# A two-layer hybrid trunk on one core: the first layer's shift and scale computed in two halves, with norm, transposes and weights placed between them

## The chip, the cores and the metric

The kernel runs on one core of a Trainium2 chip. The time is the device time of one execution in microseconds (us); the median of several executions is compared. Engine names are those of the profile: PE is TensorE's products, PEld its weight loads, DVE is VectorE, ACT is ScalarE, POOL is GpSimd, SP is the engine that issues the DMAs (SPq in the timeline, since issuing is work of its queue).

## The reference, cut to what matters

Two layers run one after the other over 1152 tokens (128 context tokens and 1024 latent tokens) of 1024 channels, in float32. At the head of each layer stands

```
m = silu(cvec) @ mod_w + mod_b          # 1024 -> 3 * 1024: shift, scale, gate
h = rmsnorm(x, norm_g) * (1 + scale) + shift
p = h @ w_in                            # one projection for all three branches
```

with one `cvec` for the context tokens and one for the latent tokens. The columns of `p` feed a windowed attention (A), a gated linear recurrence (B) and a differential attention (C), whose outputs are gated, projected, merged, projected again by `w_out` and added to `x` under `gate`. For this change only the first layer's way from `cvec` and `x` to the first columns of `p` matters.

## The kernel before, in words

**Tiling.** The 1152 tokens are nine tiles of 128 rows, handled in three chunks of three tiles. The 1024 channels are eight column blocks of 128 (`KT`, index k). `h` is kept transposed, as eight pairs `L.hh[k]`, `L.hl[k]`: each value split into a part rounded to the format of the fast products and the remainder, so that one exact product is three fast ones (`mm3`, L161 to L163 in the profile: high by high, high by low, low by high).

**Modulation of the first layer.** `mod_rows(D, b0, n)` computes n blocks of 128 columns of `m` on TensorE: four loads of 512 KB of `mod_w` (tile `modw`), eight products with 512 columns (L281; the trace shows two matmul instructions for each), one copy of the row to SBUF on ScalarE (`mrow`), four tiny transposes (L288), and two additions on VectorE into `D.modt`. It is a generator with a step per load. It is called for blocks 0 to 3 (shift, first half of the channels), 8 to 11 (scale, first half), 4 to 7 and 12 to 15 (second halves). Below, the first two calls are the first half of the modulation, the last two the second half. `mod_gs(D, k0, k1)` then makes the factor `norm_g * (1 + scale)` for column blocks k0 to k1.

**Norm.** `load_x(i)` loads one token tile (512 KB). `norm_x(c)` squares the three tiles of chunk c on ScalarE with row sums (L1142 in the profile), makes 1/sqrt by a dozen small VectorE operations (`rsqrt`, tile `rsq`), and scales the three tiles on VectorE.

**Into h.** `to_h(L, c, k, ...)` transposes column block k of the three tiles of chunk c on TensorE (three transposes, L332, into a PSUM buffer `ps_t`, of which there are three), applies factor and shift there (ScalarE, L337, or VectorE for k = 3 and 7), copies the rounded part out on ScalarE (tile `h`) and the remainder on VectorE.

**Projection weights.** `load_wu` loads three groups of 128 columns of `w_in` for all eight row blocks in nine DMAs (tile `wuraw`), and splits them into `uwh` (rounded copy, ScalarE) and `uwl` (remainder, by `split`'s last argument on VectorE or GpSimd) in three pieces. `tok_gemm(L, i, w)` then projects one token tile: for k = 0 to 7 one `mm3` into a PSUM buffer `ps_s`, of which there are four. `qkv_gemm` does so for three tiles and then copies queries, keys and values out.

**Order of the work.** The text of the kernel gives the instructions, a planner orders them. The context that the kernel is written in schedules all instructions at the end with a timeline of its own: an instruction written earlier has the higher priority (shifted where the code says `tc.high_priority`), and one that its inputs or buffers hold back can be passed by a later one. The result is a fixed order for each engine; at run time each engine takes its instructions in that order. All DMAs are issued from SP's queue. Large tiles share rings of buffers: ring S has 26 buffers, and `modw` (16 in all in this stretch), the nine tiles of `x` and the 16 tiles of `h` all come from it; ring W has 7 for the weights.

**The program's beginning, before.** The four calls of `mod_rows` stand one after the other; after the second one, tiles 0 to 2 of `x` are loaded and normalised and the first projection weights are loaded and split (`XPOS`, `WUK`). Then come both calls of `mod_gs`, the loads of tiles 3 to 8 with the rotation tables between them (`load_unit_consts`), `alloc_h`, and for each chunk its norm and eight calls of `to_h`. `unit_phase` follows with the first projection, `qkv_gemm` for unit 0.

Of the kernel before, what the change touches and what calls it, by code (L numbers as in the profile page):

```python
# [24 lines left out]
# priority offsets: attention of the units, branch products, modulation (beside the tail, w_out; its sums), recurrence  # L25
# [6 lines left out]
# chunks that branch products lag the merge; steps of the tail where they lag two  # L32
MLAG = 1
LAG2 = (7, 8)
# steps of the tail that carry a block of modulation, that carry a recurrence, that writes the states
# [3 lines left out]
# places in w_out that carry a block of modulation  # L39
MODW = ((0, 1), (0, 4), (0, 7), (1, 1), (1, 4), (1, 7), (2, 1), (2, 4))  # L40
# first layer: blocks of modulation after which the weights and the first tokens are loaded
WUK = 1
XPOS = 1
# rings of the rows of x in w_out, and in its last quarter
XT = 'EDT'
XT3 = 'ET'
# background products per group of query tiles: units of branch C, the first of them, branch A
# [3 lines left out]
# rings of shared buffers: how many of each  # L51
RINGS = {"S": 26, "P": 7, "T": 2, "Q": 2, "W": 7, "D": 3, "E": 2, "cx": 1, "tab": 1}

# columns of w_in
# [3 lines left out]
# rows of the per-layer table of short vectors  # L58
# [4 lines left out]
def hybrid_dit_kernel(ctx, tc, I, O):  # L63
# [5 lines left out]
    # buffers of each kind in PSUM  # L69
# [8 lines left out]
    def al(tag, name, *shape):  # L78
        """a buffer of one of the shared rings"""
        return big.tile([128] + list(shape), F32, tag=tag, name=name, bufs=RINGS[tag])  # L80
# [41 lines left out]
    def rsqrt(x, n, scale, eps=None):  # L122
        """1/sqrt(x*scale + eps) of a [128, n] AP, n <= 12"""
        o = tl("rsq", 4, 12, bufs=3)
        ms, y, h, t = (o[:, i, 0:n] for i in range(4))
        if eps is None:
            ts(V, ms, x, scale, ALU.mult, EPS, ALU.add)
        else:
            stt(ms, x, scale, eps, ALU.mult, ALU.add)
        ts(V, y.bitcast(I32), ms.bitcast(I32), 1, ALU.logical_shift_right)  # L130
        ts(V, y.bitcast(I32), y.bitcast(I32), -1.0, ALU.mult, float(0x5F3759DF), ALU.add)
        ts(V, h, ms, -0.5, ALU.mult)
        for _ in range(3):
            tt(V, t, y, y, ALU.mult)
            tt(V, t, t, h, ALU.mult)
            stt(y, t, 1.5, y, ALU.add, ALU.mult)
        return y

    def split(hi, lo, raw, eh="A", el="P"):
        """hi = raw rounded to fp32r, lo = raw - hi"""  # L140
        if eh == "A":
            acopy(r(hi), raw)
        else:
            V.tensor_copy(r(hi), raw)
        tt(Pq if el == "P" else V, r(lo), raw, hi, ALU.subtract)

    def ws_load(wcols, kt):
        """[kt*128, 128] weight columns -> hi, lo [128, kt, 128]"""
# [29 lines left out]
    def ws_gemm(L, wcols, consume):  # L178
        """[128 cols, tokens] = W^T h^T, per chunk of 384 tokens"""
# [5 lines left out]
    def layer_vectors(l):  # L185
        """generator: loads the rows, two per step, then turns them into columns"""
# [25 lines left out]
    def layer_scalars(D):  # L212
# [12 lines left out]
        # lamc[3] = -(e1 - e2 + lam_init)  # L225
# [11 lines left out]
        # 4*softplus(-lam) = 4*(max(-lam, 0) + log1p(exp(-|lam|)))  # L237
# [21 lines left out]
    def silu_c():  # L259
        """[128, k, s]: silu of the two conditions, latent and context, in columns"""  # L260
# [13 lines left out]
    def mod_rows(D, b0, n):  # L274
        """blocks b0 to b0 + n by TensorE: the conditions' rows, then turned into columns; a step per load"""
# [17 lines left out]
    def mod_chunk(D, b0, n, tag):  # L293
        """blocks b0 to b0 + n: products summed over row blocks by DVE, over partitions by a product with ones"""
# [22 lines left out]
    def mod_gs(D, k0, k1):  # L317
        # gs = norm_g * (1 + scale); s = 0 latent, 1 context
# [8 lines left out]
    def to_h(L, c, k, xn, tags):  # L327
        """column block k of the normalised tiles of chunk c -> h^T, hi and lo"""
# [23 lines left out]
    def load_wu(L, groups, early=False):  # L352
        """three groups of 128 columns -> (hi, lo) [128, 384] for each of the 8 row blocks"""
# [3 lines left out]
        def conv(raw):  # L357
            m = raw.shape[1]
            hi, lo = al("W", "uwh", m, 384), al("W", "uwl", m, 384)
            split(hi, lo, raw, "A", "P")  # L360
# [19 lines left out]
    def qk_rows(L, i0, pss, gains, dsts, eng=None):  # L380
        """normalise, scale and rotate pairs of heads of a few token tiles.
        gains: gain index per pair; dsts: where a pair goes, None: stays in the returned tile"""
# [41 lines left out]
    def put_k(d0, d1, p):  # L424
        """p: [head 0; head 1] -> key stacks [hi; lo] of head 0 and [lo; hi] of head 1"""
# [6 lines left out]
    def q_conv(src, nb):  # L432
        """src [128, nb, 64] -> hi and lo of the transposed blocks, each in both halves: [2, nb, 128]"""
# [11 lines left out]
    def gate_silu(L, c0, put):  # L445
        """2*silu of the gate columns from c0"""
# [19 lines left out]
    def qkv_gemm(L, u, w, gains, okey, oval, eng=None):  # L466
        """generator: emits one third of the work per step"""
# [16 lines left out]
    def k_conv(u, cache, kdst):  # L484
        """keys transposed and stacked; kdst: destinations of key blocks b0..b0+n (8: cached)"""
# [16 lines left out]
    def v_conv(u, cache, pair=False):  # L502
        """values split: hi and lo, or for a pair of heads [hi; lo] of each"""
# [19 lines left out]
    def c_probs(L, u, i, q, t):  # L523
        """unnormalised difference of the two softmaxes of q tile i -> [128, n] in a P buffer"""
# [27 lines left out]
        # softmax_0 - lam softmax_1 = (e_0 - lam l_0/l_1 e_1) / l_0; the norm after it takes 1/l_0 into its eps  # L552
# [46 lines left out]
    # key blocks (8 is the cached context) in the two key rows of a head pair, and  # L599
    # for each latent block: row, first key slot, count, first mask slot  # L600
# [40 lines left out]
    def a_probs(L, g, tiles, q):  # L641
        """softmaxes of heads 2g, 2g+1 for one or two q tiles"""
# [83 lines left out]
    def unit_phase(L):  # L726
        """the four heads of branch C, then branch A; projections run beside the attention before them"""
# [24 lines left out]
        def background():  # L752
            """projections and gates, in the order in which attention takes them"""
# [78 lines left out]
    def lru_x(L, ct):  # L832
        """input of the recurrence and its gate, to DRAM"""
# [17 lines left out]
    def lru(L, ct):  # L851
# [5 lines left out]
        # gate matrices, two 64-wide blocks on the diagonal  # L857
# [76 lines left out]
    def load_o(L, br):  # L934
        """gated branch output, hi and lo"""
# [44 lines left out]
    def tail_step(L, br, order, j, o, lag):  # L980
        """emits the products of step (br, j) one chunk at a time, branch products MLAG chunks behind the merge"""
# [22 lines left out]
    def tail_last(L, br, ohl):  # L1004
        """the last two steps of the last branch: their merge products first, so that h can go"""
# [15 lines left out]
    def gate_rows(D, q4, dst):  # L1021
        """dst [2, 256]: gate/2 in every partition, latent and context"""
# [124 lines left out]
    for n, b0 in enumerate((0, 8, 4, 12)):  # L1147
        g = mod_rows(L.D, b0, 4)
        for _ in range(3):
            drive(vec, g)  # L1150
        for _ in vec:
            pass
        drive(g)
        if n == XPOS:
            for i in range(3):
                load_x(i)
            norm_x(0)
        if n == WUK:
            L.wu = load_wu(L, c_groups(0), True)
    mod_gs(L.D, 0, 4)  # L1160
    mod_gs(L.D, 4, 8)
    for i in range(3, 9):
# [3 lines left out]
    alloc_h(L)  # L1166
    for c in range(3):
        if c:
            norm_x(c)
        for k in range(KT):  # L1170
            to_h(L, c, k, lambda t, kk, c=c: xs[3 * c + t][:, kk * 128:(kk + 1) * 128], "t")
# [49 lines left out]
def _consts():  # L1221
    """arrays that depend on shapes alone"""
# [35 lines left out]
```

## Time and profile before

| | us |
|---|---|
| median of 3 executions | 2898.65 |
| lowest, highest | 2894.25, 2900.79 |
| span of the profiled execution | 2896.5 |
| TensorE busy in it | 2741.7 (95%) |
| VectorE, ScalarE, GpSimd busy | 1753.5, 1272.5, 908.3 |

The page gives no time for the profiled execution other than its span, from the first instruction to the last; it lies 2.15 us below the median. In a timeline each row has the start, the time during which instructions of this group ran, engine, line, operation, output and inputs, shape and count; brackets hold the idle time of the engine just before and what ended it. A row of a table by windows has the busy time of each engine (with its number of instructions) in the stretch, the granted TensorE clock (1.00 is the upper of two levels, 2.4 GHz, 0.50 the lower, 1.2 GHz), the busy share of the DMA engines and the bytes they moved.

### The profile page before, as it was taken

What the parts mean: (1) busy time and instruction counts of PE and PEld (TensorE: products, weight loads), DVE (VectorE), ACT (ScalarE), POOL (GpSimd) and SP (SyncE); (2) the same over time, 40 slices, a digit from 0 to 9 for tenths busy, and PEclk for the clock granted to TensorE, in tenths of its full rate; (3) what the DMA queues carried; (4) which work ended last, traced back from release to release, by engine and by line L of the source; (5) the groups of instructions that cost most, each with busy time, mean ns of one, the idle gap of its engine ahead of it and who ended that gap; (6) DMA issues with size and microseconds to landing.
All of it is one profiled execution on the core that took longest, in us unless ns stands there. A gap on an engine that the chain in (4) does not pass through costs nothing.

```text
span 2896.5 us, 44162 instructions
## 1 busy us (share of the span) xinstructions
PE 2741.7 (95%) x16745; PEld 2651.9 (92%) x16745; DVE 1753.5 (61%) x4388; ACT 1272.5 (44%) x2569; POOL 908.3 (31%) x700
## 2 busy tenths in 40 slices
PE   8999999999997989998999999999999989899999
PEld 4989999999997989998999899998999979899989
DVE  5797878776536455116967887787665455311162
ACT  4464555566654531212144645555666446212110
POOL 1243344531234342213103343445212333322230
PEclk9999999999999999999999999999999999999999
DMA  6011011012221133114630110110112222311122
GB/s 227 25 33 32 21 32 42 31 52 73 67 75 62 58 128 108 49 41 140 191 107 25 33 34 19 33 48 31 55 63 80 66 66 64 110 41 52 48 89 85
DMA packets 231697, 190.74 MB, mean 66 GB/s; under 512 B 21746, under 2 KB 217660, under 8 KB 231484
## 3 DMA queue, kind: packets, MB, share of 16 engines
q1 hardware_dynamic: 231484, 187.92, 20.5%
q8 instruction: 132, 2.16, 0.3%
q14 instruction: 81, 0.66, 0.1%
HBM read 153.52 MB, written 34.35 MB: 65 GB/s over the span
## 4 chain that ended last, share of the span: by engine, by line
PE 47%; DVE 9%; ACT 3%; issue 2%; DMA 2%; POOL 1%; SPq 0%; DVEq 0%; POOLq 0%; ACTq 0%
PE ps_s L161 13%; PE ps_s L162 13%; PE ps_s L163 13%; DVE macc L110 2%; PE ps_o L709 1%; DVE lr L110 1%; PE ps_t L700 1%; DMA modw<-in_mod_w_dram 1%; DVE P L540 1%; PE ps_t L567 1%; PE ps_s L538 1%; PE ps_s L539 1%; DVE lu L110 1%; POOL li L101 0%; PE ps_s L660 0%
## 5 line engine op out<-in xcount | busy, mean ns | idle before, releaser
L161 PE MATMUL ps_s<-h,wsh 128*128 128x384 f32 x1920 | 661.1, 344 | 52.4 <-DVE yr L110 46.3
L163 PE MATMUL ps_s<-h,wsl 128*128 128x384 f32 x1920 | 655.3, 342 | 0.9 <-POOL wsl L101 0.9
L162 PE MATMUL ps_s<-h,wsh 128*128 128x384 f32 x1920 | 655.2, 341 | 0.0
L161 PEld LDWEIGHTS ps_s<-h,wsh 128*128 128x128 f32 x1920 | 364.7, 190 | 59.1 <-DVE yr L110 48.3
L163 PEld LDWEIGHTS ps_s<-h,wsl 128*128 128x128 f32 x1920 | 363.8, 190 | 2.0 <-POOL wsl L101 1.6
L162 PEld LDWEIGHTS ps_s<-h,wsh 128*128 128x128 f32 x1920 | 364.5, 190 | 0.6
L101 POOL TENSOR_TENSOR wsl<-wsraw,wsh 128x1024 fp32r<-128x1024 f32 x80 | 198.6, 2482 | 386.9 <-ACT wsh L98 184.1
L161 PE MATMUL ps_s<-uwh,h 128*128 128x384 f32 x864 | 297.6, 347 | 4.7 <-ACT h L98 2.1
L162 PE MATMUL ps_s<-uwl,h 128*128 128x384 f32 x864 | 294.9, 343 | 0.1
L163 PE MATMUL ps_s<-uwh,h 128*128 128x384 f32 x864 | 292.9, 345 | 0.0
L110 DVE SCALAR_TENSOR_TENSOR ps_s<-mg,ps_s 128x384 f32<-128x384 f32 x96 | 52.9, 559 | 353.2 <-PE ps_s L163 353.2
L101 POOL TENSOR_TENSOR qkraw<-qkraw,tab 128x384 f32<-128x384 f32 (+2 forms) x92 | 132.0, 1446 | 342.7 <-DVE qkraw L101 228.6
L540 DVE TENSOR_SCALAR_CACHE_REDUCE P<-ps_s 128x384 f32<-128x384 f32 (+1 forms) x400 | 205.5, 539 | 41.0 <-PE ps_s L539 40.0
L101 DVE TENSOR_TENSOR PT<-ps_t,PT 128x512 fp32r<-128x512 f32 (+2 forms) x304 | 187.6, 625 | 59.2 <-ACT PT L98 57.4
L161 PE MATMUL ps_s<-oh,wb 128*128 128x384 f32 x576 | 194.1, 347 | 26.3 <-DVE yr L101 9.4
L98 ACT ACTIVATE PT<-ps_t 128x512 fp32r<-128x512 f32 (+2 forms) x304 | 159.7, 546 | 124.3 <-PE ps_o L163 66.5
L550 ACT ACTIVATE P<-P,csm 128x1152 f32<-128x1152 f32 (+1 forms) x144 | 165.8, 1155 | 97.9 <-DVE csm L105 97.9
L957 ACT ACTIVATE mg<-ps_s 128x384 f32<-128x384 f32 x144 | 69.8, 486 | 307.2 <-PE ps_s L163 176.6
L162 PE MATMUL ps_s<-ol,wb 128*128 128x384 f32 x576 | 194.5, 344 | 0.0
L163 PE MATMUL ps_s<-oh,wb 128*128 128x384 f32 x576 | 194.3, 344 | 0.0
L161 PE MATMUL ps_s<-woh,yh 128*128 128x256 f32 x576 | 166.5, 290 | 11.8 <-DVE xt L101 6.5
L161 PEld LDWEIGHTS ps_s<-uwh,h 128*128 128x128 f32 x864 | 165.0, 191 | 8.5 <-DVE P L540 3.0
(252 smaller groups left out, 6320.8 us busy)
## 6 DMA issues: line engine op xcount, KB each, us to landing
wsraw<-in_w_in_dram SPq DMA_DIRECT2D x80, 512.0 KB, 3.7
wuraw<-in_w_in_dram SPq DMA_DIRECT2D x72, 192.0 KB, 3.5
ol<-osp SPq DMA_DIRECT2D x24, 576.0 KB, 3.8
modw<-in_mod_w_dram SPq DMA_DIRECT2D x16, 512.0 KB, 6.0
woraw<-in_w_out_dram SPq DMA_DIRECT2D x16, 512.0 KB, 4.4
modw<-in_mod_w_dram SPq DMA_DIRECT2D x14, 576.0 KB, 5.5
modw<-in_mod_w_dram SPq DMA_DIRECT2D x19, 384.0 KB, 4.1
wuraw<-in_w_in_dram SPq DMA_DIRECT2D x36, 128.0 KB, 2.3
```

Source lines behind the costliest of these rows:

```text
L98: A.activation(out=out, in_=in_, func=AF.Copy, scale=scale)
L101: e.tensor_tensor(out=out, in0=a, in1=b, op=op)
L110: V.scalar_tensor_tensor(out=out, in0=a, scalar=s, in1=b, op0=op0, op1=op1)
L161: T.matmul(out=out, lhsT=r(lh), rhs=r(rh), start=first, stop=False)
L162: T.matmul(out=out, lhsT=r(lh), rhs=r(rl), start=False, stop=False)
L163: T.matmul(out=out, lhsT=r(ll), rhs=r(rh), start=False, stop=last)
L538: T.matmul(out=p, lhsT=qh, rhs=kk, start=True, stop=False)
L539: T.matmul(out=p, lhsT=ql, rhs=kk, start=False, stop=True)
L540: V.tensor_scalar(out=S[:, n * c:n * c + n], in0=p, scalar1=1.0, scalar2=NEG, op0=ALU.mult, op1=ALU.max, accum_out=mx[:, mp, c:c + 1])
L550: A.activation(out=Ss[mp][:, 0:n], in_=Ss[mp][:, 0:n], func=AF.Exp, scale=0.125, bias=nm[:, mp:mp + 1], accum_out=acc)
L567: T.transpose(p[:, b, j * 128:(j + 1) * 128], Pm[:, (b0 + b) * 128:(b0 + b + 1) * 128], ident)
L957: A.activation(out=m, in_=p, func=AF.Tanh, scale=0.5)
```

## The change

The text of the program's beginning is put in another order. The first two calls of `mod_rows` run as before. Then come `mod_gs` for the first four column blocks, loads and norm of tiles 0 to 2, `alloc_h`, `to_h` of chunk 0 for k = 0 to 3, and the first projection weights; then the other two calls of `mod_rows`, `mod_gs` for the last four blocks, `to_h` of chunk 0 for k = 4 to 7, the loads of tiles 3 to 8, and chunks 1 and 2 as before. In `load_wu` with `early` (this one call) the remainder `uwl` is made on VectorE where it was made on GpSimd. Nothing in `unit_phase` or behind it is edited. The rest of the diff removes comments and the two constants.

```
-# first layer: blocks of modulation after which the weights and the first tokens are loaded
-WUK = 1
-XPOS = 1
...
         def conv(raw):
             m = raw.shape[1]
             hi, lo = al("W", "uwh", m, 384), al("W", "uwl", m, 384)
-            split(hi, lo, raw, "A", "P")
+            split(hi, lo, raw, "A", "V" if early else "P")
             return [(hi[:, j, :], lo[:, j, :]) for j in range(m)]
...
-    for n, b0 in enumerate((0, 8, 4, 12)):
-        g = mod_rows(L.D, b0, 4)
+    def first_h(c, ks):
+        for k in ks:
+            to_h(L, c, k, lambda t, kk: xs[3 * c + t][:, kk * 128:(kk + 1) * 128], "t")
+
+
+    gens = [mod_rows(L.D, b0, 4) for b0 in (0, 8, 4, 12)]
+    for g in gens[:2]:
         for _ in range(3):
             drive(vec, g)
         for _ in vec:
             pass
         drive(g)
-        if n == XPOS:
-            for i in range(3):
-                load_x(i)
-            norm_x(0)
-        if n == WUK:
-            L.wu = load_wu(L, c_groups(0), True)
     mod_gs(L.D, 0, 4)
+    for i in range(3):
+        load_x(i)
+    norm_x(0)
+    alloc_h(L)
+    first_h(0, range(4))
+    L.wu = load_wu(L, c_groups(0), True)
+    for g in gens[2:]:
+        for _ in g:
+            pass
     mod_gs(L.D, 4, 8)
+    first_h(0, range(4, 8))
     for i in range(3, 9):
         load_x(i)
         if i == 5:
             load_unit_consts(L)
-    alloc_h(L)
-    for c in range(3):
-        if c:
-            norm_x(c)
-        for k in range(KT):
-            to_h(L, c, k, lambda t, kk, c=c: xs[3 * c + t][:, kk * 128:(kk + 1) * 128], "t")
+    for c in (1, 2):
+        norm_x(c)
+        first_h(c, range(KT))
```

## Rows read from the trace of the kernel before

**Rows 1.** Part 1 of the page: TensorE's busy time over the span.
```profile
PE 2741.7 (95%) x16745; PEld 2651.9 (92%) x16745; DVE 1753.5 (61%) x4388; ACT 1272.5 (44%) x2569; POOL 908.3 (31%) x700
```

**Rows 2.** Table by windows, from 24 to 60 us.
```profile
24.00:28.00 4.00, 1.00 (x9) 0.64 (x8) 3.77 (x12) 3.22 (x6) 2.77 (x2) 0.80 1.04 344
28.00:32.00 4.00, 3.83 (x5) 0.59 (x6) 3.93 (x3) 0.72 (x1) 3.92 (x2) 0.50 1.05 399
32.00:36.00 4.00, 4.00 (x9) 0.72 (x8) 3.79 (x17) 0.00 (x0) 0.30 (x1) 0.85 1.05 389
36.00:40.00 4.00, 4.00 (x10) 0.77 (x9) 3.22 (x20) 1.60 (x3) 0.00 (x0) 1.00 1.04 409
40.00:44.00 4.00, 4.00 (x14) 0.94 (x13) 0.71 (x7) 2.44 (x6) 0.00 (x0) 1.00 0.72 172
44.00:48.00 4.00, 2.53 (x16) 1.34 (x14) 1.97 (x14) 1.99 (x5) 0.00 (x0) 1.00 0.50 182
48.00:52.00 4.00, 2.91 (x13) 2.76 (x14) 3.49 (x8) 4.00 (x9) 0.00 (x0) 0.79 0.93 312
52.00:56.00 4.00, 4.00 (x23) 3.90 (x21) 3.18 (x20) 3.45 (x9) 0.00 (x0) 0.79 0.41 114
56.00:60.00 4.00, 4.00 (x28) 3.93 (x27) 3.77 (x10) 2.81 (x6) 0.00 (x0) 1.00 0.07 20
```

**Rows 3.** Timeline, 28 to 35 us: products of the modulation's second half, at both clock levels.
```profile
28.17 12.11 PE L281 MATMUL ps_s<-modw,sc 128*2 128x512 f32 x22 [2.08 <-DMA modw<-in_mod_w_dram]
...
28.98 0.13 PEld L281 LDWEIGHTS ps_s<-modw,sc 128*2 128x2 f32 x1 [0.72 <-issue]
29.83 0.13 PEld L281 LDWEIGHTS ps_s<-modw,sc 128*2 128x2 f32 x1 [0.73 <-issue]
...
33.67 0.09 PEld L281 LDWEIGHTS ps_s<-modw,sc 128*2 128x2 f32 x1 [0.34 <-issue]
34.10 0.09 PEld L281 LDWEIGHTS ps_s<-modw,sc 128*2 128x2 f32 x1 [0.34 <-issue]
```

**Rows 4.** Timeline, 45 to 49.1 us: from the last modulation row to the first projection.
```profile
45.03 0.59 ACT L98 ACTIVATE mrow<-ps_s 2x512 f32<-2x512 f32 x1 [2.02 <-PE ps_s L281]
...
45.67 0.41 PE L288 MATMUL ps_t<-ident,mrow 2*128 2x2 f32 x4 [0.68 <-ACT mrow L98]
...
46.01 1.20 PE L332 MATMUL ps_t<-ident,x 128*128 128x128 f32 x9
...
46.59 2.04 ACT L337 ACTIVATE ps_t<-ps_t,modt,gs 128x128 f32<-128x128 f32 x5 [0.98 <-DVE gs L110]
...
48.53 0.51 ACT L98 ACTIVATE h<-ps_t 128x384 fp32r<-128x384 f32 x1
...
49.09 0.44 PE L161 MATMUL ps_s<-uwh,h 128*128 128x384 f32 x1 [1.88 <-ACT h L98]
```

**Rows 5.** Timeline, 23 to 35 us: norm of chunk 0 and the remainder of the weights.
```profile
23.65 0.17 DVE L107 TENSOR_SCALAR rsq<-ssq 128x3 f32<-128x3 f32 x1 [7.39 <-ACT xsq L1142]
...
24.78 0.15 DVE L110 SCALAR_TENSOR_TENSOR rsq<-rsq 128x3 f32<-128x3 f32 x1
...
25.23 7.07 POOL L101 TENSOR_TENSOR uwl<-wuraw,uwh 128x1152 fp32r<-128x1152 f32 x3 [24.79 <-ACT uwh L98]
25.36 2.50 DVE L110 SCALAR_TENSOR_TENSOR rsq<-rsq 128x3 f32<-128x3 f32 x1
...
32.38 2.06 DVE L105 TENSOR_SCALAR x<-x,rsq 128x1024 f32<-128x1024 f32 x3
```

**Rows 6.** The instructions of tile ol: a 128x1152 subtraction on VectorE.
```profile
L101 DVE TENSOR_TENSOR ol<-ol,oh x12: 1335/1356/2710, 728.6 to 2644.2; 128x1152 fp32r<-128x1152 f32 x12
```

**Rows 7.** Timeline: projection products at the upper level, and chunk 0's first value copied out.
```profile
60.31 0.34 PE L161 MATMUL ps_s<-uwh,h 128*128 128x384 f32 x1
60.48 0.34 PE L162 MATMUL ps_s<-uwl,h 128*128 128x384 f32 x1
...
66.23 0.27 ACT L98 ACTIVATE uvr<-ps_s 128x128 f32<-128x128 f32 x1
```

**Rows 8.** Timeline of SP's queue and of ScalarE: loads of x behind those of the modulation.
```profile
28.14 3.11 SPq L95 DMA_DIRECT2D x<-in_x_sample_dram  x3
...
38.99 1.06 ACT L1142 ACTIVATE xsq<-x 128x1024 f32<-128x1024 f32 x1 [0.67 <-DMA x<-in_x_sample_dram]
```

**Rows 9.** Waits of TensorE, whole span: two of those behind the beginning.
```profile
PE ps_s L161 <- DVE yr L110: 55.6, 10, 8.8
...
PE ps_t L493 <- DVE ukr L101: 2.7, 1, 2.7
```

## The prediction

> **What bounds the kernel now.** I read the page's first part, then a table by windows of the beginning, then the timeline of the same stretch, engine by engine. TensorE is busy for 95% of the span [rows 1], so the kernel is a TensorE queue with holes, and a change in the beginning can only be worth what it closes of holes and slow clock there. The reader should see four stretches in the table [rows 2]. From 24 to 28 us TensorE runs 1.00 of 4 us. From 28 to 44 it is full, with products of the modulation's second half. From 44 to 52 it has holes again (2.53 and 2.91 of 4). From 52 on it is full. The granted clock is low twice: 0.80, 0.50 and 0.85 from 24 to 36, and 0.79 twice from 48 to 56, each time after TensorE had stood idle. The DMA engines are full until 40 us, at 340 to 409 GB/s, so nothing big can be loaded earlier.
>
> The ceiling follows from these rows. Idle time is 3.00 + 0.17 + 1.47 + 1.09 = 5.73 us. The slow clock costs busy time times the missing share: 3.83 x 0.50 + 4.00 x 0.15 = 2.5 us in the first slow stretch, 2 x 4.00 x 0.21 = 1.7 us (an upper bound, for the idle part counts too) in the second. Together 9.9 us, 0.34% of the span. More than that the change can't give in the beginning.
>
> **Why the second half of the modulation is TensorE's and not the DMA's.** Its first product waits for a load until 28.17 [rows 3]; from then on the weight loads follow one another by 0.85 us at the low clock (28.98, 29.83) and by 0.43 us at the full one (33.67, 34.10), which is the ratio of the two levels. So the products set the pace: 32 x 0.43 = 13.8 us at full clock, and 2.5 us more for the slow start, which gives 28.17 + 16.3 = 44.5, near the 45.0 at which the row is copied [rows 4]. A load of 524 KB at some 390 GB/s arrives every 1.34 us, and four instructions take 1.72.
>
> **The change, part by part.**
>
> *Norm and transposes of chunk 0, k = 0 to 3, ahead of the second half.* Four times three transposes leave the stretch behind the modulation. Nine cost 1.20 us there [rows 4], so one is 0.13 and twelve are 1.6 us at full clock. They need the normalised x. Its row sums are there at 23.65 and it was ready only at 34.4, for VectorE's small steps stretched from 0.15 to 2.50 us while GpSimd made `uwl` (25.23 to 32.3) [rows 5]. With GpSimd silent, some twelve steps of 0.15 and the scaling of 2.06 end near 27.5. VectorE can slip one or two of the `uwl` pieces between (1.36 each for the large ones [rows 6], 3.6 for all three with the smaller in proportion), so 27.5 to 30.2. I take 27.5, since the steps are written ahead of the weights. Then 0.7 us of the hole before 28.17 takes transposes and the other 0.9 us delays the modulation. Bounds: 0 if all fits the hole, 2.4 if all twelve run at the low clock (3.1 us less 0.7).
>
> *Factor, shift and split of these four blocks* are ScalarE and VectorE work (about 1.5 us of ScalarE for each block, by the 2.04 and 0.51 us rows [rows 4]). ScalarE is nearly idle from 28 to 36 (0.72 and 0.00 of 4 us) [rows 2], so I cost it at nothing. Without this cover it would be 6 us, on the chain.
>
> *`uwl` on VectorE* adds 3.6 us to VectorE and removes 7.07 from GpSimd [rows 5, 6]. The first projection product that needs it comes after 46; VectorE's filler until 40 (small steps of the next stage) can wait. Cost nothing, gain nothing of its own: x at 34.4 would also have been early enough for the end at 46, not for the hole at 28.
>
> *Projection of chunk 0 over k = 0 to 3.* Three tiles x four blocks x three products = 36 products, started 0.17 us apart [rows 7], 6.2 us. They have the lowest priority, and the modulation's products are always ready, so I expect them behind the modulation, from 46.1, when the last tiny transposes (45.67 + 0.41) are out [rows 4]. There TensorE waited for chunk 0's `h` until 49.09. That is the gain: 49.09 - 46.08 = 3.0 us of hole in which before only transposes ran, of which three more are already done (12 instead of 9, 0.4 us). The 6.2 us of products last until some 52.3, past the first converted block of k = 4 to 7 (near 48.5, as now), so no new hole opens, and the idle time that preceded the second slow stretch is gone: 1.7 us, between 0 (the clock falls all the same) and 1.7.
>
> *Buffers and loads.* `h` takes 16 of ring S's 26 buffers before the second half of `modw` asks for 8, and x holds 3. So the eighth `modw` and the tiles 3 to 8 of x wait for earlier `modw` to be used, at one per 1.7 us from 30 on. SP issues in order, so the tables behind them wait too. But the DMA engines have a backlog until 40 us, and tiles 3 to 5 reached ScalarE at 38.99 although issued at 28.14 [rows 8]. They would be issued at about 33 to 37 and land at 39 to 42, as now. Cost 0 (bounds 0 and 2 us, the hole if chunk 1 is late; chunk 0's products last until about 60).
>
> **Sum.** -3.0 - 0.4 - 1.7 + 0.9 = -4.2 us. Behind it the work is the same, and TensorE's queue is full from 52 on, so the shift should reach the end. The page gives only the span, 2896.5, which becomes 2892.3. The median stands 2.15 us above it: 2898.65 - 4.2 = **2894.4 us**. With the bounds above the forecast's own range is 2890 to 2898. 0.2%, about what a measurement of this kernel can tell from no change, is 5.8 us.
>
> **Rivals.**
>
> 1. *The first slow stretch goes too, or TensorE has room between the modulation's products.* If TensorE is at work soon enough after 24.6 to keep the full clock, 2.5 us more are saved, and the delay of 0.9 turns to nothing: -7.6 us. If the partial products fit into gaps of the modulation, the end is earlier by up to the ceiling. Time 2889 to 2891. For it: the weight path is busy only 0.6 to 0.9 of 4 us from 28 to 44 [rows 2]. Against it: x is ready at 27.5 at the earliest, 3 us after the last product, and the pace follows the clock, so the array itself is what is full. The Trainium skill (Trainium Kernel Development and Optimization, Performance Expectations) says that matmul busy time is a poor measure of how near the limit TensorE is, because matmuls are pipelined, and that the busy share of weight loads is a good one. By that rule, with 0.6 to 0.9 of 4 us of weight loads, the second half would leave room for the 6.2 us and the time would be near 2889; by the row with the two paces it leaves none. I follow the row. Chance 0.17.
>
> 2. *The partial products go between those of the modulation without room, or the planner leaves the order as it was.* The modulation then ends up to 6.2 us later, nothing is left to fill the wait of 3.0 us behind it, and what remains is the transposes: -1.5 to 0 us, 2897 to 2899. For it: in the trace of before the normalised x waited from 34.4 to 46.0 for its transposes, so the order is the planner's and not the data's. Chance 0.20.
>
> 3. *Slower: TensorE waits at the head of the second half.* The planner has its own times. If in TensorE's queue the transposes for k = 3 and the first partial products stand ahead of modulation products whose data is there, TensorE stands still for the chain x, transpose, factor, split, `uwl`. It needs one of three `ps_t` buffers to come back, and ScalarE and VectorE work on four blocks until about 27.5 + 6 = 33.5 to 35. Up to 7 us from 28.17 on, and the gain of 4.2 is then only the 1.5 of rival 2, since the products are used up. Time up to 2898.65 + 7 - 1.5 = 2904; it decides the sign once the standstill is over 1.5 us, and it is a measurable loss from 7.3 on. For it: queues are in order, and the row at 46.01 shows transposes issued three blocks at a time, by buffers. Against it: the second half's products are ready early, and a planner passes what is not ready. Chance 0.15.
>
> The forecast keeps 0.48. Behind the beginning the planner's order can also change; one of the waits that TensorE has there, 2.7 us for the first keys or up to 8.8 for a merge [rows 9], can come or go. It has no sign, and widens every case by some 3 us.
>
> **How the numbers follow.** Faster by over 0.2% means below 2892.9: a third of the forecast with its widening (0.17), nearly all of rival 1 (0.16) and a little of rival 2 (0.04): 0.38 with rounding up. Slower by over 0.2%, above 2904.4: half of rival 3 and the tails of the others: 0.14. The rest, 0.48, is within. The range reaches from rival 1's middle, widened, to rival 3: 2886 to 2903.
>
> **What would show it.** Right: transposes of x (L332) near 27 to 30 us, the second half's last row copied at 45 to 46, projection products (L161) directly behind the tiny transposes at 46, a clock of 1.00 from 48 to 56, chunk 0's values copied out at about 62 instead of 66.23 [rows 7], no GpSimd work from 25 to 32. Projection products between 28 and 45 with the row copied at 50 would mean rival 2; a gap of TensorE after 28 with a load already there, rival 3. Wrong in principle: chunk 0 out 4 us earlier and the end not, which would mean that a later wait on VectorE takes the gain.

## The result, and the profile after

The changed kernel takes 2921.7 us (median of 4 runs, 2917.8 to 2926.6) against 2899.4 us for the kernel before in the same comparison (2894.3 to 2900.8): ratio 1.0084, interval 1.0069 to 1.0100. It is slower by 20 to 29 us by the interval (the medians are 22.3 apart). The forecast, 2894.4, and its range, 2886 to 2903, are missed on the wrong side, and none of the rivals goes as far.

The profiled execution has a span of 2916.0 us against 2896.5, 19.5 more. TensorE's busy time is what it was [rows 1], so the loss is idle time. Part 1 of the page of the kernel after:

```profile
PE 2741.8 (94%) x16745; PEld 2650.6 (91%) x16745; DVE 1745.0 (60%) x4391; ACT 1271.8 (44%) x2569; POOL 906.5 (31%) x697
```

The table by windows of the kernel after shows where it lies; these rows answer to [rows 2].

```profile
24.00:28.00 4.00, 0.57 (x7) 0.40 (x6) 3.86 (x19) 3.10 (x4) 0.00 (x0) 1.00 1.00 254
28.00:32.00 4.00, 1.72 (x8) 1.40 (x9) 3.62 (x14) 0.00 (x0) 0.00 (x0) 0.62 0.24 55
32.00:36.00 4.00, 0.51 (x3) 0.11 (x1) 1.33 (x9) 2.53 (x7) 0.00 (x0) 0.50 0.62 170
36.00:40.00 4.00, 0.90 (x3) 0.50 (x3) 2.71 (x6) 1.79 (x5) 0.00 (x0) 0.50 0.25 57
40.00:44.00 4.00, 2.38 (x3) 0.34 (x4) 0.31 (x1) 0.00 (x0) 0.00 (x0) 0.50 1.04 397
...
76.00:80.00 4.00, 0.00 (x0) 0.00 (x0) 2.23 (x10) 3.94 (x8) 0.00 (x0) 0.59 0.00 0
80.00:90.00 10.00, 6.37 (x23) 5.69 (x24) 9.82 (x42) 4.92 (x10) 0.00 (x0) 0.50 0.00 0
```

TensorE stands nearly idle from 24 to 41, and again from 74.6 to 81.8. The last column but one is the answer: from 28 to 40, where the DMA engines were full before (1.05, 1.05, 1.04), their share is 0.24, 0.62 and 0.25. The loads are not slow, they have not been asked for. The timeline of SP's queue in the kernel after says what SP did instead; the last row answers to [rows 8]:

```profile
12.66 10.59 SPq L92 DMA_DIRECT2D wuraw<-in_w_in_dram  x9
23.29 0.47 SPq L92 DMA_DIRECT2D tab<-in_ropecos_dram  x1
...
30.56 1.44 SPq L92 DMA_DIRECT2D wuraw<-in_w_in_dram  x3
34.24 0.34 SPq L92 DMA_DIRECT2D kc<-in_cache_c_k_dram  x1
34.68 0.30 SPq L92 DMA_DIRECT2D rows<-in_norm_g_dram  x1
...
37.48 0.25 SPq L92 DMA_DIRECT2D rows<-in_subln_c_dram  x1
37.77 4.28 SPq L92 DMA_DIRECT2D modw<-in_mod_w_dram  x8
47.40 11.37 SPq L92 DMA_DIRECT2D x<-in_x_sample_dram  x6
```

In the kernel before, SP's queue has the same loads here, beside the three tiles of x in [rows 8]:

```profile
23.75 4.21 SPq L95 DMA_DIRECT2D modw<-in_mod_w_dram  x8
...
43.04 1.38 SPq L95 DMA_DIRECT2D x<-in_x_sample_dram  x3
```

Tables, the weights of the next projection, cached keys and the vector rows of the next layer are issued first, and SP stands still between 32.0 and 34.2. The eight `modw` of the second half come at 37.77 (before: 23.75), and tiles 3 to 8 of x at 47.40 (before: three at 28.14, three at 43.04), one at a time over 11 us, since each takes the buffer of a `modw` that has just been used. The waits of SP's queue say so (engine, line, what for, us, times, longest):

```profile
SPq L92 <- PE ps_s L278: 13.3, 6, 4.4
```

The `modw` wait for nothing of the kind: the `h` block of k = 3, the last ahead of them in the program, is written until 40.3, behind their issue. They stand where the planner put them in SP's queue. The timelines of TensorE and ScalarE show the two consequences:

```profile
30.28 2.23 PE L329 MATMUL ps_t<-ident,x 128*128 128x128 f32 x9 [4.71 <-DVE x L102]
...
37.19 0.90 PE L329 MATMUL ps_t<-ident,x 128*128 128x128 f32 x3 [4.68 <-DVE h L98]
...
41.62 10.90 PE L278 MATMUL ps_s<-modw,sc 128*2 128x512 f32 x20 [3.53 <-DMA modw<-in_mod_w_dram]
...
60.16 0.59 ACT L95 ACTIVATE mrow<-ps_s 2x512 f32<-2x512 f32 x1 [8.74 <-PE ps_s L278]
...
70.95 1.05 ACT L1139 ACTIVATE xsq<-x 128x1024 f32<-128x1024 f32 x1
...
74.25 0.28 ACT L95 ACTIVATE uvr<-ps_s 128x128 f32<-128x128 f32 x1 [2.16 <-PE ps_s L160]
...
75.52 1.10 ACT L1139 ACTIVATE xsq<-x 128x1024 f32<-128x1024 f32 x1
...
77.30 1.09 ACT L1139 ACTIVATE xsq<-x 128x1024 f32<-128x1024 f32 x1
...
81.79 2.15 PE L329 MATMUL ps_t<-ident,x 128*128 128x128 f32 x9 [7.23 <-DVE x L102]
...
103.22 0.27 ACT L95 ACTIVATE uvr<-ps_s 128x128 f32<-128x128 f32 x1
```

The first product of the second half is at 41.62 instead of 28.17 [rows 3], the last modulation row is copied at 60.16 instead of 45.03 [rows 4]: 15.1 us late. Of this 7.1 come back, because twelve transposes and ten of the 36 partial products (52.45 to 54.38) are done by then and the other 26 keep TensorE at work behind it, at a clock of 1.00 from 60 to 72: the values of chunk 0 are copied out at 74.25 instead of 66.23 [rows 7], 8.0 late. Then TensorE waits 7.23 us for x of chunk 1, and the granted clock is down at 0.50 (1.2 GHz) from 80 to 90, behind that standstill. Chunk 1's values come at 103.22; before, at 81.21. That is 22.0 late, and chunk 2 is late by the same 22.0 (118.19 against 96.17). The profiled execution ends 19.5 us late, so these 22 us reach the end nearly whole.

This second wait is not one for bytes. The six tiles of x have all come by 64:

```profile
64.00:68.00 4.00, 2.59 (x20) 2.07 (x19) 0.74 (x5) 2.79 (x8) 0.00 (x0) 1.00 0.00 0
```

The DMA share is 0.00 there, and ScalarE's list of waits has none for these tiles. Their squares (`xsq` at 70.95, 75.52 and 77.30) come late because ScalarE takes its instructions in a fixed order, in which two of the three stand behind the copies of chunk 0's values. No trace shows the planner's own times, which make this order; in e2 below the loads of x are early, and the squares are early with them.

**Two theories** were put to the test. *L, late loads:* the planner hands out the buffers of a ring in the order of the program. `h` now asks for 16 buffers of ring S ahead of the second `modw`, so the loads of `modw`, and behind them of x, are planned only when the first `h` has been, and SP's queue is filled with later work meanwhile. *Q, the queues of the engines:* what costs is the new order on TensorE and VectorE, as rival 3 had it (TensorE stands on the chain x, transpose, factor, split, `uwl`), whatever the loads do.

### The profile page after: what moved, and what is told of

It is laid out like the page before. It is cut to its first block, busy times and chain, and to the rows that moved or that the text cites. A ratio compares the mean times of both kernels' runs of the same rounds, so it can differ in the third digit from the quotient of the medians.

```text
span 2916.0 us, 44158 instructions
## 1 busy us (share of the span) xinstructions
PE 2741.8 (94%) x16745; PEld 2650.6 (91%) x16745; DVE 1745.0 (60%) x4391; ACT 1271.8 (44%) x2569; POOL 906.5 (31%) x697
## 4 chain that ended last, share of the span: by engine, by line
PE 68%; DVE 17%; ACT 6%; issue 4%; DMA 3%; POOL 2%; SPq 1%; DVEq 0%; ACTq 0%; POOLq 0%
PE ps_s L158 17%; PE ps_s L159 17%; PE ps_s L160 17%; DVE macc L107 2%; PE ps_o L706 2%; DVE lr L107 2%; DVE P L537 2%; PE ps_t L697 2%; PE ps_s L535 1%; PE ps_t L564 1%; PE ps_s L536 1%; DVE lu L107 1%; DMA modw<-in_mod_w_dram 1%; POOL li L98 1%; DVE PT L98 1%
```

## The experiments

Each run is compared with the kernel before, run beside it on the same chip. "mrow" is the start of the copy of the modulation's last row, "values" the start of the copy of the first value tile of chunks 0, 1 and 2, all in us in the profiled execution; the change of the end is the ratio and its interval taken on that comparison's median of the kernel before.

```
run                          mrow    values 0 / 1 / 2          end: ratio [interval]            us
before                       45.03   66.23 /  81.21 /  96.17
after                        60.16   74.25 / 103.22 / 118.19   1.0084 [1.0069, 1.0100]   +24.4
e1 modw in another ring      45.47   60.48 /  89.77 / 104.74   1.0032 [1.0020, 1.0045]    +9.3
e2 x in another ring         66.32   81.80 /  96.78 / 111.73   1.0049 [1.0031, 1.0066]   +14.2
e3 loads written first       46.24   63.50 /  78.37 /  94.03   0.9995 [0.9986, 1.0004]    -1.4
e4 before, uwl on VectorE    43.99   65.14 /  80.11 /  95.07   1.0010 [1.0001, 1.0019]    +2.9
e5 after, uwl on GpSimd      64.22   78.30 / 107.16 / 122.12   1.0115 [1.0100, 1.0131]   +33.3
e6 before, modw loads late   52.71   72.25 /  87.22 / 102.18   1.0031 [1.0021, 1.0041]    +9.0
e7 all modw loads first      38.38   65.31 /  80.29 /  95.25   0.9992 [0.9983, 1.0001]    -2.3
e8 weights behind all modw   38.09   63.69 /  78.37 /  94.03   0.9991 [0.9982, 1.0000]    -2.6
e9 weights behind 3/4        41.21   63.72 /  78.41 /  94.06   0.9994 [0.9985, 1.0003]    -1.7
e10 e3, weights behind modw  39.46   56.71 /  71.46 /  87.29   0.9972 [0.9962, 0.9982]    -8.1
```

The column of chunk 2 and the end agree within 4 us everywhere but in e5 (7 us apart): what happens before 100 us is what the end shows. Behind it, the wait for the first keys [rows 9] is there in every kernel looked at (2.49 after, 3.25 in e3 and e8, 3.26 in e10).

**e1: the second-half modw in ring P (one in Q).** Nothing is moved in the program; only the ring differs.

```
-    def mod_rows(D, b0, n):
+    def mod_rows(D, b0, n, tags="SSSS"):
...
-            w = al("S", "modw", 2, 128 * n)
+            w = al(tags[k0 // 2], "modw", 2, 128 * n)
...
+    gens = [mod_rows(L.D, b0, 4, t) for b0, t in ((0, "SSSS"), (8, "SSSS"), (4, "PPPP"), (12, "PPPQ"))]
```

> Theory L (late loads): in the changed kernel the loads of the modulation's second half stand in SP's queue behind the tables, the next weights and the next layer's rows (issued at 37.77 us, before at 23.75), because ring S gives out its buffers in the order of first use and h comes first; and the tiles 3 to 8 of x stand behind that again. This run takes only the first: those eight loads get buffers of other rings. L expects them issued near 24 us, the last modulation row copied at 45 to 48 us (changed kernel 60.2), chunk 0's first value copied out at 60 to 64 us (74.25), but chunk 1's still 25 to 30 us behind it, since x is still late; time 2903 to 2911. Rival Q (TensorE's queue): the loss is the standstill behind transposes and partial products that stand among the modulation's products, with the weights' remainder on VectorE stretching the norm; then the loads do not matter and the time stays at 2915 or more.

SP's queue in e1:

```profile
23.86 4.23 SPq L92 DMA_DIRECT2D modw<-in_mod_w_dram  x8
...
48.25 3.28 SPq L92 DMA_DIRECT2D x<-in_x_sample_dram  x6
```

The loads are back at 23.86 and the last row at 45.47, at the same place in the program as in the kernel after. So it is the ring, not the place of the loads, that holds them. Too few buffers alone (16 + 3 + 8 asked of 26) would hold the eighth load, not all eight. 15 of the 24 us are gone. Tiles 3 to 8 of x still take buffers of ring S and are still issued at 48; chunk 0 is early by 5.8 us and chunk 1 late by 8.6, with the squares of its second and third tile again behind chunk 0's values (61.76 and 63.53, after 60.48). Theory L's range holds; Q's (2915 and more) does not.

**e2: tiles 3 to 8 of x in ring P, modw left in S.**

```
-        xs[i] = al("S", "x0", 1024)
+        xs[i] = al("S" if i < 3 else "P", "x0", 1024)
```

> The other half of the loss alone: in the changed kernel only the tiles 3 to 8 of x get buffers of another ring, so that they can be loaded early; the loads of the modulation's second half stay late. L expects those loads still issued at 36 us or later, chunk 0's first value copied out at 72 to 78 us, chunk 1's some 15 us behind it (changed kernel 29), time 2903 to 2910. Q expects 2915 or more, since TensorE's queue up to chunk 0 is the same.

SP's queue in e2:

```profile
24.16 1.42 SPq L92 DMA_DIRECT2D x<-in_x_sample_dram  x3
...
33.24 1.38 SPq L92 DMA_DIRECT2D x<-in_x_sample_dram  x3
...
43.81 4.26 SPq L92 DMA_DIRECT2D modw<-in_mod_w_dram  x8
```

Now x is early and the chunks follow one another by 15 us, as in the kernel before: the 14 us that chunk 1 had lost beyond that came of the late x (the squares of tiles 3 to 5 start at 28.61 here, of tiles 6 to 8 at 38.38). Expected of chunk 0 was 72 to 78, and it came at 81.80, with the end above its range: `modw` goes out at 43.81, 6 us later than in the kernel after, since the x loads and the small loads stand ahead of it in SP's queue. What e1 takes away (15.1 us) and what e2 does (10.2) add up to 25.3; both together, in e3, take away 25.8. That the two add up is in part chance, since e2's 10.2 is what is left after `modw` has become later still.

**e3: all loads written ahead of the first use of h.** The rest of the change stays: norm, transposes and partial products of chunk 0 first, `uwl` on VectorE.

```
     norm_x(0)
+    L.wu = load_wu(L, c_groups(0), True)
+    w2 = {b0: [mod_load(L.D, b0, 4, 2 * i, t) for i, t in enumerate(tags)]
+          for b0, tags in ((4, "PPPP"), (12, "PPPQ"))}
+    for i in range(3, 9):
+        load_x(i)
+        if i == 5:
+            load_unit_consts(L)
     alloc_h(L)
     first_h(0, range(4))
...
+        for _ in mod_rows(L.D, b0, 4, w2[b0]):
```

> Both parts taken: the loads of the modulation's second half (in other rings) and of tiles 3 to 8 of x are written ahead of h, all else of the change stays (early norm, early transposes and projection of k = 0 to 3, the remainder on VectorE). L expects the order of loads of the kernel before, the last modulation row at 45 to 47 us, chunk 0 out at 60 to 64 us (before 66.23) and chunk 1 at 75 to 79 (before 81.21); the predicted gain of 4 us then shows: 2890 to 2898. Q expects the standstill to stay: 2908 or more.

`mod_load` holds the two lines of `mod_rows` that allocate and load a `modw`; `tags` are those of e1. This is the kernel that the prediction described. Tiles 3 to 5 of x stay in ring S as in e1, but are written ahead of `h`, and are issued at 28.16 instead of 48.25: within one ring the place in the program decides. Windows of e3:

```profile
28.00:32.00 4.00, 4.00 (x5) 0.57 (x6) 4.00 (x11) 0.00 (x0) 0.00 (x0) 0.50 1.05 407
...
44.00:48.00 4.00, 4.00 (x19) 1.92 (x16) 1.87 (x12) 1.40 (x3) 0.00 (x0) 1.00 0.67 218
48.00:52.00 4.00, 4.00 (x26) 3.68 (x26) 3.83 (x14) 2.68 (x5) 0.00 (x0) 1.00 0.80 266
52.00:56.00 4.00, 3.84 (x25) 3.53 (x24) 2.48 (x16) 3.65 (x10) 0.00 (x0) 1.00 0.42 117
```

TensorE is full where it had 2.53 and 2.91 of 4 us [rows 2], and the second slow stretch is gone. Chunk 0's values come 2.7 us earlier than before (the sum said 4.2). The end is not told apart from that of the kernel before: the interval reaches from 4.1 us faster to 1.2 us slower.

**e4: the kernel before with uwl on VectorE.** The change's second edit alone.

```
-            split(hi, lo, raw, "A", "P")
+            split(hi, lo, raw, "A", "V" if early else "P")
```

> One part alone: the kernel before with the remainder of the first weights on VectorE instead of GpSimd, nothing else. L expects no difference that can be told, within 4 us of the kernel before, with x normalised several us earlier than 34.4. Q, as far as it puts the loss on VectorE, expects 5 us or more slower.

Chunk 0 is 1.1 us earlier, the end later by 0.3 to 5.5 us by the interval, and no row of the beginning accounts for that. It is no part of a loss of 24, and nothing of a gain.

**e5: the change with uwl on GpSimd again** (the same two lines, the other way).

> The changed kernel with the remainder uwl made on GpSimd again; nothing else is edited. Late loads (theory L): the second-half modw is still issued near 38 us and tiles 3 to 8 of x near 47, so nothing of the loss comes back; x of chunk 0 is normalised later (32 to 36 instead of 31.5), first h later by as much, 2917 to 2927 us. Theory Q (uwl's pieces on VectorE, slipped between the steps of the norm, hold up the head of the second half): at least half of the loss of 22 comes back, 2900 to 2911 us.

Q expected half of the loss back; instead the kernel is 9 us slower than the change, and 3 above L's range. VectorE in e5:

```profile
30.68 1.77 DVE L98 TENSOR_TENSOR rsq<-rsq 128x3 f32<-128x3 f32 x1
...
32.51 0.15 DVE L107 SCALAR_TENSOR_TENSOR rsq<-rsq 128x3 f32<-128x3 f32 x1
...
32.80 2.06 DVE L102 TENSOR_SCALAR x<-x,rsq 128x1024 f32<-128x1024 f32 x3
```

A step of three columns takes 1.77 us while GpSimd works, as in [rows 5], so x is normalised 3.3 us later than after (32.80 against 29.47), the first transposes come at 33.59, and the second `modw` is issued at 40.33, 2.6 us later. The link is in SP's queue: it waits 4.6 us (1.1 after) for VectorE to clear the buffer into which the next layer's rows are loaded, which VectorE does behind the norm, and the `modw` stand behind these rows. Tiles 3 to 8 of x, expected near 47, come from 51.44 on. In the changed kernel the head of the beginning delays the loads, and so everything. VectorE was the better place for `uwl` here.

**e6: a dose of late loads in the kernel before.** Order of the program as before, but tiles 3 to 8 of x are loaded ahead of the second `modw`.

```
         if n == XPOS:
             for i in range(3):
                 load_x(i)
             norm_x(0)
+            for i in range(3, 9):
+                load_x(i)
...
-    for i in range(3, 9):
-        load_x(i)
-        if i == 5:
-            load_unit_consts(L)
+    load_unit_consts(L)
```

> The kernel before, with the order of its program kept except that tiles 3 to 8 of x (3.1 MB) are loaded ahead of the second-half modw, so that those come later by nothing but the transfers ahead of them: 3.1 MB at some 0.39 MB per us is 8 us. A dose of late modulation loads alone, with none of the change's order of norm, transposes and projection. Theory L: first product of the second half at 34 to 37 us instead of 28.2, last mrow copied at 51 to 54 instead of 45.0, chunk 0's values copied out at 73 to 76 instead of 66.2, the next two 15 us apart (x is there), the end later by 5 to 9 us: 2900 to 2905. Theory Q (what costs is the order of TensorE's queue and not the loads): the end within 3 us of the kernel before.

The `modw` goes out at 31.02 (7.3 us late) and the first product starts at 35.77 (7.6 late):

```profile
35.77 16.86 PE L281 MATMUL ps_s<-modw,sc 128*2 128x512 f32 x32 [10.38 <-DMA modw<-in_mod_w_dram]
```

The first weights move with them (issued from 20.68 instead of 13.18) and are split by 39.6, well ahead of the first projection. The last row is 7.7 us late, all three chunks 6.0 (72.25, just under the 73 to 76 that was expected), the end 6 to 12, with the median of 2905.2 at the top of its range. So a delay of loads alone, without any of the change's new order, costs nearly its own length. That is theory L without the change.

**e7: all sixteen modw ahead of x and the weights**, in the kernel before with `uwl` on VectorE: a version that follows from L.

```
-WUK = 1
-XPOS = 1
+WUK = 3
+XPOS = 3
```

> A version that follows from theory L: the kernel before with x of chunk 0 and the projection weights loaded behind all sixteen modw instead of between the two halves, and uwl on VectorE. The modw of the second half come without x and weights (1.6 MB and 1.2 to 4.7 MB) ahead of them. Theory L: first product of the second half at 22 to 25 us, last mrow copied at 38 to 41 instead of 45.0; chunk 0's values copied out at 60 to 64 if weights and x land by 43, and the end 2 to 6 us earlier, 2890 to 2894. If the weights become the late load (uwh and uwl ready only after 46), chunk 0 stays at 65 to 68 and the end within 3 us of the kernel before.

The modulation behaves as expected (second half from 24.01 without a wait, last row at 38.38, 6.7 us early), and chunk 0 gains 0.9. The late load is not the weights but x of chunk 0: its squares start at 30.58 instead of 19.88, and TensorE waits for the normalised x until 41.71.

**e8 and e9: x between the halves as before, the weights behind all sixteen modw (e8) or behind twelve (e9).** `WUK = 3` and `WUK = 2` in e4's kernel, nothing else.

> The kernel before with the first projection's weights loaded behind all sixteen modw instead of between the halves (x of chunk 0 stays between them, where e7 moved it too), and uwl on VectorE. 1.6 MB less ahead of the second-half modw is 4 us at some 0.39 MB per us, so the first product of the second half should come at 24.5 to 26 us instead of 28.2, with no idle stretch long enough to lower the clock, the last mrow be copied at 39 to 41 instead of 45.0, and x be normalised by 31. Theory L (what is loaded late sets the beginning): first projection at 43 to 45 us instead of 49.1, chunk 0's values copied out at 60 to 62 instead of 66.2, and the end 4 to 6 us earlier, 2891 to 2895. If the weights land too late (after 41): chunk 0 at 63 to 66 as in e7, the end within 3 us of the kernel before. Theory Q has no gain here: within 3 us.

> As e8, with the weights between the third and the last quarter of modw. 4 us of loads ahead of the last quarter alone, whose products start some 7 us after the third's: first product of the second half at 24.5 to 26 us, last mrow at 39.5 to 42, weights there by 36. Theory L: first projection at 43.5 to 46, chunk 0's values at 60.5 to 63, the end 3 to 6 us earlier than before, 2892 to 2896; better than e8 by up to 2 us if the weights are late there.

In e8 the second half starts at 23.14, x is normalised by 27.4, the last row is copied at 38.09 and the first projection starts at 44.21, all as expected or better. Chunk 0 comes at 63.69 all the same, 2.5 us early instead of 4 to 6; e9 is the same at 63.72. Windows of e8:

```profile
40.00:44.00 4.00, 0.52 (x3) 0.31 (x3) 0.31 (x3) 4.00 (x10) 0.00 (x0) 1.00 0.69 166
44.00:48.00 4.00, 3.79 (x14) 3.69 (x15) 3.62 (x17) 1.38 (x4) 0.00 (x0) 0.57 0.64 209
52.00:56.00 4.00, 2.86 (x16) 2.51 (x17) 3.34 (x20) 3.97 (x12) 0.00 (x0) 1.00 0.06 14
```

With early loads, ScalarE is the next limit: from 40 to 44 it is busy 4.00 of 4 us with factor, shift and split of chunk 0 and the squares of tiles 3 to 5, while TensorE has 0.52. Theory L's sizes for chunk 0 and for the end are missed in both (e9's chunk 0 and end each by under 1 us); loads alone don't carry further than 2 or 3 us.

**e10: e3 with the weights loaded behind the second modw.** One line of e3 moved down.

```
     norm_x(0)
-    L.wu = load_wu(L, c_groups(0), True)
     w2 = {b0: [mod_load(L.D, b0, 4, 2 * i, t) for i, t in enumerate(tags)]
           for b0, tags in ((4, "PPPP"), (12, "PPPQ"))}
+    L.wu = load_wu(L, c_groups(0), True)
     for i in range(3, 9):
```

> e3 (the change with all loads written ahead of the first use of h) with the weights loaded and converted behind the second-half modw and tiles 3 to 8 of x. First product of the second half at 24.5 to 26 us, last mrow at 39 to 43. Theory L: the weights are now the last load, behind 1.6 + 4.2 + 3.1 MB, and land near 44 to 47; the partial products of k = 0 to 3 start there instead of at 46.1, so chunk 0's values come at 62 to 66 against 63.5 in e3, and the end is within 3 us of e3. If the planner moves tiles 3 to 8 of x behind the weights, chunk 0 is at 59 to 61 and the end 3 to 5 us earlier than e3.

The planner did what the last sentence of the expectation allows for: it put the weights (23.61 to 34.05) ahead of tiles 3 to 8 of x, so that SP's order is that of e8 within 1 us. Windows of e10:

```profile
32.00:36.00 4.00, 4.00 (x12) 0.99 (x13) 1.89 (x11) 3.97 (x10) 0.00 (x0) 1.00 1.12 324
40.00:44.00 4.00, 4.00 (x27) 3.73 (x26) 2.47 (x6) 3.66 (x8) 0.00 (x0) 1.00 0.68 159
44.00:48.00 4.00, 4.00 (x29) 3.89 (x29) 3.00 (x19) 2.01 (x5) 0.00 (x0) 1.00 0.64 222
52.00:56.00 4.00, 3.80 (x25) 3.41 (x24) 2.99 (x17) 3.50 (x9) 0.00 (x0) 1.00 0.10 22
```

and its timeline where the modulation ends:

```profile
39.36 0.55 PE L333 MATMUL ps_t<-ident,x 128*128 128x128 f32 x3
39.84 0.41 PE L289 MATMUL ps_t<-ident,mrow 2*128 2x2 f32 x4
40.17 0.79 PE L158 MATMUL ps_s<-uwh,h 128*128 128x384 f32 x3
```

TensorE is full at a clock of 1.00 from 20 to 80 but for 0.2 us. ScalarE makes `h` for k = 0 to 2 from 32.5 to 37 beside the modulation's products, and the partial products follow at 40.17 without a gap. Chunk 0's values come at 56.71, 9.5 us early (59 to 61 was expected for this order), and the kernel takes 2889.9 us (2886.2 to 2893.5): 0.9972 of the kernel before, 5 to 11 us faster. With loads in the same order e8 gains 2.6 and e10 8.1, so the order that the change introduces is worth some 5.5 us (8.1 - 2.6; the two intervals, 0 to 5 and 5 to 11, just meet; chunk 0 differs by 7.0) once its loads are not held back. e10 is the fastest kernel of the study.

## Why the prediction was wrong

**The step that failed is "Buffers and loads", costed at 0 with bounds of 0 and 2 us.** It counted buffers (16 for `h`, 3 for x, so that 7 of 8 `modw` would fit) where the order decides, and had tiles 3 to 8 of x issued at 33 to 37; they came from 47.40 on. By e1, with the same program text and another ring, all eight go out at 23.86; in ring S behind `h` all eight go out at 37.77. The step saw the order of SP's queue only for the tables behind the loads, and not that tables, keys and rows of the next layer would be issued ahead of them. Its cover was "the DMA engines have a backlog until 40 us". That backlog consisted of the very loads that the change holds back: with them gone the share is 0.24 to 0.62. A backlog covers a later issue only if it is other work. The bound of 2 us should have been the whole length of the delay; e6 shows what that is worth: 7.7 us of the modulation's delay became 6.0 in each chunk and 6 to 12 at the end. Most of +24 comes from this step: e1 (the `modw`) takes 15 away, e2 (x) 10, e3 (both) 26.

**The norm, at 27.5 (27.5 to 30.2 as bounds), ended at 31.5.** I took 27.5 "since the steps are written ahead of the weights", but the planner did not keep to that. VectorE's timeline after has all three `uwl` pieces between the steps:

```profile
24.93 1.36 DVE L98 TENSOR_TENSOR uwl<-wuraw,uwh 128x1152 fp32r<-128x1152 f32 x1
26.20 0.15 DVE L98 TENSOR_TENSOR rsq<-rsq 128x3 f32<-128x3 f32 x1
...
28.21 0.95 DVE L98 TENSOR_TENSOR uwl<-wuraw,uwh 128x768 fp32r<-128x768 f32 x1
...
29.47 2.08 DVE L102 TENSOR_SCALAR x<-x,rsq 128x1024 f32<-128x1024 f32 x3
```

The size of a piece was right (1.36). In e10, where the weights arrive later, x is scaled from 26.03 to 28.2, 0.7 behind the predicted time. In e3 the norm is as late as in the kernel after (the scaling begins at 29.87), so no transposes fit ahead of 28: nine of the twelve stand between the modulation's products and cost their full time, and three come behind (47.27).

**The gain itself was there.** 3.0 us of hole behind the modulation, 0.4 of transposes and 1.7 of slow clock, less 0.9, made 4.2; e3 shows TensorE full from 44 on, the clock at 1.00 and chunk 0 early by 2.7. The last row is copied 1.2 late there instead of 0.9, and from it to the values 3.9 are saved instead of 5.1. At the end of the kernel this gain is not told from nothing (e3). The first slow stretch (0.50 from 28 to 32) stays, as the forecast had it. *Behind the beginning* little changes, as was argued: chunk 2 and the end move by nearly the same.

**The rivals.** Rival 3 named the symptom (TensorE stands still at the head of the second half) with a chance of 0.15, but its mechanism was TensorE's queue with the data there, and at most 7 us. In the trace after TensorE does stand on x (4.71) and on `h` (4.68), but with no `modw` there to pass to; the wait that ends last is for the load, and e5 and e6 speak against the engines' order as its cause. The mark that was set, "a gap of TensorE after 28 with a load already there", is thus not met. That a load is held behind an allocation was no rival. Rival 1's room between the products is not there: in e10 the second half lasts from 23.64 to 39.36, 15.7 us, which is 32 products (14.1), nine transposes of chunk 0 (1.3) and one group of tiny ones (0.3). The Trainium skill (Trainium Kernel Development and Optimization, Performance Expectations) names the busy share of weight loads, beside the share of peak throughput, as the good measure of how near its limit TensorE is. Here that share is 0.99 of 4 us in e10 from 32 to 36, and each added transpose still makes the stretch longer by its own time; the measurement decides against the busy share of weight loads for products of two weight columns. Rival 2 came about in small part and not as a cause: after, ten of the 36 partial products stand between the modulation's, which had become late; in e3 and e10 none does (they begin at 46.13 and 40.17, behind the modulation's last).

## What to carry to other kernels

Where buffers are handed out in the order of the program, writing a compute tile ahead of a load of the same ring makes the load wait for it, and loads that are needed later pass (37.77 instead of 23.75 here). What needs a late load can also be placed late in its engine's order, where the early arrival of the bytes no longer helps: the second wait, 7.23 us, ended at 81.79, with x there since 64 at the latest. Before computation is moved ahead, write out the loads that it passes and the ring each takes its buffer from, then move the loads first. And ask of a busy DMA stretch whose bytes it carries: it didn't hide a delay of those same bytes here.

## What the runs showed that was not expected

SP's queue is filled with loads of far later use once an early load is held: 25 loads, those of the next layer among them, stand between the first weights and the `modw` of 37.77. In e2, freeing x made `modw` 6 us later still.

A standstill costs twice. In e6 TensorE has no work from 25.4 to 35.8; the granted clock is 0.50 from 32 to 40 and 0.78 from 40 to 44, so that the first products behind the wait run at the lower level. In the kernel after it is 0.50 from 80 to 90, behind 7.2 us of waiting, where projection products of chunk 1 start 0.32 us apart instead of 0.17 [rows 7]. In e10, where TensorE hardly stops, it is 1.00 from 20 to 90.

What stays open: what the loads of `modw` would do in ring S if only written ahead of `h`, and how the planner's own times put the squares of chunk 1 where they are; why e5's end is 7 us later than its chunk 2 accounts for, and why e4's end tends to be later though its beginning is earlier. No run was made for any of these.
